# Weight groups multiplied by halves of the model's width over two PSUM banks, in a two-layer hybrid decoder step

## The chip, the cores and the metric

The kernel runs on one core of one Trainium2 chip. The metric is the device time of one execution in microseconds (us). TensorE (PE in the rows; its weight loads are PEld) multiplies into PSUM, VectorE (DVE), ScalarE (ACT) and GpSimd (POOL) do the elementwise work, and SyncE (SP) and ScalarE issue the DMAs.

## The reference

One inference step of a decoder with two layers. 2048 prompt tokens (one sequence) and 8 single sample tokens go through each layer with the same weights. Cut to what matters here:

```
hn   = rms_norm(x, norm_w)                     # (T, 1024)
proj = hn @ w_in                               # (T, 3336), split into 15 parts
       # r_q r_k r_v r_g | m_q m_k m_v m_o m_g m_i m_f | s_u s_g | a_q a_g   (256 wide; m_i, m_f 4 each)
ret  = head_norm(retention(rope(r_q), rope(r_k), r_v)) * silu(r_g)
ml   = head_norm(mlstm(m_q, m_k, m_v, m_i, m_f) * sigmoid(m_o)) * silu(m_g)
s5   = glu(gelu(s5_scan(s_u) + d * s_u)) * silu(s_g)
xa   = softmax(a_q @ mem_k.T / 8) @ mem_v * silu(a_g)
y    = x + concat(ret, ml, s5, xa) @ w_out     # (T, 1024)
# after the last layer: rms_norm(y, final_norm_w)
```

The outputs are y for prompt and sample tokens, the new recurrent states, and the memory keys and values. All is f32.

## The kernel before, in words

**Units and groups.** The prompt is cut into 4 units of 512 tokens, so there are 8 units in all (layer, unit). Each unit's normalised input stands transposed in SBUF as hT, the model's width on the partitions in 8 slices k of 128. The weights come in 140 groups of 256 columns (one, m_v, of 264), in an order written out by hand (ORDER and `wstream`): 4 groups for the memory, 13 projection groups for each unit, 4 groups of w_out (out0 to out3) for each unit, the last set of these by a function of its own (`out_last`).

**A group's weights.** `wload` brings a group as four quarters q0 to q3 of 256 rows (tiles wraw, four buffers, DMAs on SP's queue). `wsplit` makes of each quarter a rounded part whi on ScalarE and the rest wlo = wraw - whi, on VectorE for q0 and q2 and on GpSimd for q1 and q3. whi and wlo have WB = 6 buffers each: the four quarters of the current group and two of the next. `advance(i, 0)` loads group i+1 if that has not been done and splits its first half; `advance(i, 1)` splits its second half and loads group i+2.

**A group's matmuls.** A product takes three matmuls for each slice k: high with high, high with low, low with high. `tok_bank` puts tokens on the partitions (two token tiles of 128 in one PSUM bank; 256 columns each matmul, 96 matmuls for a group), `feat_bank` puts the group's columns on the partitions (512 tokens to a matmul, 48 for a group). In both, a bank takes all eight slices k, so q0 to q3 in turn, before the next bank m of the group begins. The banks pm come from a pool of four. After each bank its result is taken out of PSUM (`evac`, `evac_f`, or the add onto xr in `group_out`) and the function yields; then every open side chain makes one step (`step_sides`). Side chains (S5 scan, mLSTM, retention, attention, gates, norms) have four PSUM banks ps of their own and put their small matmuls and transposes between those of the groups.

**Unit b = 1 of each layer** carries the 8 sample tokens as well; there the feature groups run in two pieces of 260 columns. The last group of a unit is r_g; after each of its banks the next unit's input xt is transposed and split into hT (`hn_T`, two token tiles of 128 after each bank), and the next unit begins with m_v, whose banks take one token tile each.

**Who sets the order.** The program is written by the functions above, and a scheduler then places each engine's instructions in an order of its own; each engine runs its list strictly in that order. `group_out` before it starts makes side steps until all six parts of the unit's mix are there (mixd).

Of the kernel before, what the change touches and what calls it, by code (L numbers as in the profile page):

```python
# [7 lines left out]
F32 = mybir.dt.float32  # L8
# [4 lines left out]
OP = mybir.AluOpType  # L13
# [13 lines left out]
UT = 512  # L27
# [90 lines left out]
class Builder:  # L118
# [93 lines left out]
    def setup(self):  # L212
        nc, I, cp = self.nc, self.I, self.cp
        c = lambda n, s, dt=F32: cp.tile(s, dt, name=n, tag=n)
# [3 lines left out]
        self.mem_load()  # L218
        self.wload(0)
        self.hnl = self.hn_load(0, 0)  # L220
        next(self.hnl)
        self.wload(1)
        self.maskb = c("maskb", [128, 512], BF16)
# [84 lines left out]

    def wload(self, i):
        if i >= len(self.wseq) or i in self.wraw:  # L310
            return
        src, segs = self.wsegs(i)
        v = src.rearrange("(k p) c -> p k c", p=128)
        r = []
# [7 lines left out]
        self.wraw[i] = (r, o)  # L322

    def wsplit(self, i, half):
        if i >= len(self.wseq):
            return
        hi, lo, done = self.wspl.setdefault(i, ([], [], set()))
        if half in done:
            return
        done.add(half)  # L330
        r, n = self.wraw[i]
        for q in (2 * half, 2 * half + 1):
            hi.append(self.wp.tile([128, 2, 264], F32R, name=self.nm("whi"), tag="whi", bufs=WB))
            lo.append(self.wp.tile([128, 2, 264], F32R, name=self.nm("wlo"), tag="wlo", bufs=WB))
            h = hi[q][:, :, :n]
            self.act(h, r[q][:, :, :n])
            e = self.nc.gpsimd if q % 2 else self.nc.vector
            e.tensor_tensor(lo[q][:, :, :n], r[q][:, :, :n], h.bitcast(F32), OP.subtract)  # L338

# [48 lines left out]

    def tok_bank(self, tiles, n, hi, lo, aT, ps=None):

        ps = ps or self.mbank()
        for x, sl in enumerate(tiles):
            o = ps[:, x * n:(x + 1) * n]
            for k in range(8):
                a, c = aT(0, k, sl), aT(1, k, sl)
                h = hi[k // 2][:, k % 2, :n]
                self.mm(o, a, h, k == 0, False)
                self.mm(o, a, lo[k // 2][:, k % 2, :n], False, False)
                self.mm(o, c, h, False, k == 7)
        return ps  # L400

    def feat_bank(self, m, hi, lo, cols):

        ps = self.mbank()[:, :cols.stop - cols.start]
        for k in range(8):
            wh, wl = [x[k // 2][:, k % 2, m * 128:(m + 1) * 128] for x in (hi, lo)]
            self.mm(ps, wh, self.hT[0][:, k, cols], k == 0, False)
            self.mm(ps, wh, self.hT[1][:, k, cols], False, False)
            self.mm(ps, wl, self.hT[0][:, k, cols], False, k == 7)
        return ps  # L410
# [4 lines left out]
    def group(self, i):  # L415
        kind, l, b, g = self.wseq[i]
        if i == 0:
            self.wsplit(0, 0)
            self.wsplit(0, 1)
        hi, lo, _ = self.wspl[i]  # L420
        if kind == "mem":
# [10 lines left out]
        elif g in FEAT:  # L432
            if g == "r_q":
                for m in range(2):
                    self.u["rq", m] = self.g4([128, 2, UT], n="rqt")
                    self.dmaa(self.u["rq", m], self.I["c_rq"][b, m])
            smp = self.sample_in_unit(kind, l, b)
            pieces = [(0, 260), (260, 520)] if smp else [(0, UT)]
            for m in range(2):
                for c0, c1 in pieces:  # L440
                    ps = self.feat_bank(m, hi, lo, slice(c0, c1))
                    c2 = min(c1, UT)
                    self.evac_f(l, b, g, m, ps[:, :c2 - c0], slice(c0, c2))
# [6 lines left out]
                    if c1 >= UT and m == 1:  # L450
                        self.advance(i, 1)
                    yield
        else:
            if g == "m_v":
                jobs = [[t] for t in range(4)]
            else:
                jobs = [[0, 1], [2, 3]]
            n = 264 if g == "m_v" else 256
            for m, ts in enumerate(jobs):
                sls = [slice(t * 128, (t + 1) * 128) for t in ts]  # L460
                ps = self.tok_bank(sls, n, hi, lo, self.hslice)
                self.evac(l, b, g, m, ps)
                if m in (0, len(jobs) - 1):
                    self.advance(i, min(m, 1))
                if g == "r_g":
                    nxt = self.next_unit(l, b)
                    if nxt:
                        self.hn_T(2 * m)
                        self.hn_T(2 * m + 1)
# [4 lines left out]
    def advance(self, i, half):  # L474
        if half == 0:
            self.wload(i + 1)
            self.wsplit(i + 1, 0)
        else:
            self.wsplit(i + 1, 1)
            self.wload(i + 2)  # L480

# [236 lines left out]
    def gate_mix(self, u, l, b, src, g, br, gn, m):  # L718
# [6 lines left out]
        hi, lo = self.mix_tiles(u, br)  # L725
# [6 lines left out]
        for kk in range(2):  # L732
# [4 lines left out]
                                           h_.bitcast(F32), op0=OP.mult, op1=OP.subtract)  # L737
        u["mixd"] = u.get("mixd", 0) + 1

# [638 lines left out]
    def group_out(self, i, l, b, g, hi, lo):  # L1378
        v = self.nc.vector
        u = self.units[l, b]  # L1380
        while u.get("mixd", 0) < 6:
            n = u.get("mixd", 0)
            self.step_sides()
# [4 lines left out]

        if l == self.depth - 1 and b == self.NU - 1:
            yield from self.out_last(i, l, b, g, hi, lo, src, aT)  # L1390
            return
        for m in range(2):
            t0 = b * UT + m * 256
            xr = self.tb([128, 2, 256], "xr", bufs=2)
            rows = lambda a: a[t0:t0 + 256, g * 256:(g + 1) * 256].rearrange("(t p) c -> p t c", p=128)
            self.dma(xr, rows(src))
            ps = self.tok_bank([slice(t * 128, (t + 1) * 128) for t in (2 * m, 2 * m + 1)], 256, hi, lo, aT)
            v.tensor_tensor(xr, xr, ps.rearrange("p (t c) -> p t c", t=2), OP.add)  # L1398
            self.dma(rows(self.xd[l]), xr)
            self.advance(i, m)  # L1400
            yield
# [532 lines left out]
```

## Time and profile before

| what | value |
|---|---|
| median of 3 runs | 2450.93 us (2448.82 to 2454.46) |
| the profiled execution's own time | 2451.49 us |
| its span, first to last instruction | 2449.7 us |
| mean granted TensorE clock | 0.946 |
| busy: PE / PEld / DVE / ACT / POOL | 89% / 81% / 68% / 40% / 35% |
| mean DMA rate | 135 GB/s |

Busy PE counts the run-in and run-out of each pipelined matmul, so it stands above the time in which columns stream. The granted clock is 1.0 at 2.4 GHz and 0.5 at 1.2 GHz, and a mean of 0.946 mixes the two.

### The profile page before, as it was taken

The page shows a single profiled execution, that of the slowest core. Times are in us where ns is not written, and L with a number is a line of the kernel's source. Part 1 is how long each engine was busy: PE and PEld are TensorE (multiplying, and loading weights), DVE is VectorE, ACT ScalarE, POOL GpSimd, SP SyncE. Part 2 cuts the span into 40 slices and gives each one's busy share as a digit, 9 for nine tenths or more (in the row PEclk, how much of TensorE's full clock was granted, in tenths as well). Part 3 has the DMA queues.
Part 4 walks back from the last instruction along what each step waited for, and adds up shares of the span by engine and source line. Part 5 has one row for each costly group of instructions (what it writes and reads, how often), then busy time and mean ns, then how long its engine had stood idle before and what let it go on. Part 6 is the DMA issues. An engine that isn't in the chain of part 4 may idle for free.

```text
span 2449.7 us, 44181 instructions
## 1 busy us (share of the span) xinstructions
PE 2175.0 (89%) x16130; PEld 1989.2 (81%) x16130; DVE 1663.0 (68%) x4003; ACT 978.3 (40%) x2152; POOL 845.2 (35%) x755
## 2 busy tenths in 40 slices
PE   7899957897889989987889999878989899999898
PEld 6788856897788878875888889777989787888788
DVE  7987835646675789773874767347576678868474
ACT  4554423342433544243442454223443354433343
POOL 2443312232233435442322343213332244434243
PEclk9999988899999999998999999888999999999899
DMA  7525374447374435735435442784446643573522
GB/s 222 168 86 179 99 109 96 132 137 94 88 208 130 127 115 171 217 99 102 121 110 178 118 132 77 171 183 87 87 101 208 198 125 113 161 247 121 101 64 105
DMA packets 355529, 329.78 MB, mean 135 GB/s; under 512 B 109144, under 2 KB 310040, under 8 KB 355312
## 3 DMA queue, kind: packets, MB, share of 16 engines
q1 hardware_dynamic: 329472, 266.53, 43.2%
q10 hardware_dynamic: 25840, 60.43, 7.8%
q8 instruction: 127, 2.08, 0.4%
q14 instruction: 90, 0.74, 0.1%
HBM read 265.40 MB, written 45.73 MB: 127 GB/s over the span
## 4 chain that ended last, share of the span: by engine, by line
PE 34%; DVE 15%; DMA 14%; issue 3%; ACT 2%; SPq 2%; POOL 1%; ACTq 0%; DVEq 0%; POOLq 0%
PE pm L180 24%; PE ps L180 8%; DMA sv<-t 4%; DMA wraw<-w_in 3%; PE ps L184 2%; DVE wlo L338 2%; SPq L190 2%; DVE sm L207 1%; DVE t L1302 1%; DMA X<-ud 1%; DMA s5im_p<-xprev 1%; DVE sm L206 1%; DVE sm L208 1%; DMA ud<-U 1%; DVE sv L1297 1%
## 5 line engine op out<-in xcount | busy, mean ns | idle before, releaser
L338 POOL TENSOR_TENSOR wlo<-wraw,whi 128x512 fp32r<-128x512 f32 (+1 forms) x280 | 400.5, 1435 | 655.9 <-ACT whi L187 513.7
L180 PE MATMUL pm<-hT,whi 128*128 128x512 f32 (+1 forms) x2240 | 610.1, 361 | 5.3 <-ACT whi L187 5.3
L180 PE MATMUL pm<-whi,hT 128*128 128x256 f32 (+1 forms) x3072 | 593.4, 289 | 16.3 <-ACT whi L187 13.7
L180 PEld LDWEIGHTS pm<-whi,hT 128*128 128x128 f32 x3072 | 488.8, 193 | 23.1 <-ACT whi L187 14.3
L187 ACT ACTIVATE whi<-wraw 128x512 fp32r<-128x512 f32 (+1 forms) x560 | 342.2, 629 | 392.1 <-PE pm L180 250.2
L180 PE MATMUL pm<-wlo,hT 128*128 128x256 f32 (+1 forms) x1536 | 440.8, 288 | 28.3 <-DVE wlo L338 27.1
L180 PEld LDWEIGHTS pm<-hT,whi 128*128 128x128 f32 x2240 | 397.4, 194 | 64.5 <-ACT whi L187 5.7
L180 PE MATMUL pm<-hT,wlo 128*128 128x512 f32 (+1 forms) x1120 | 398.0, 359 | 25.7 <-DVE wlo L338 24.3
L180 PE MATMUL pm<-whi,mix 128*128 128x256 f32 x2048 | 382.1, 286 | 9.1 <-ACT whi L187 5.5
L338 DVE TENSOR_TENSOR wlo<-wraw,whi 128x512 fp32r<-128x512 f32 (+1 forms) x280 | 248.7, 891 | 153.2 <-ACT whi L187 130.7
L180 PEld LDWEIGHTS pm<-whi,mix 128*128 128x128 f32 x2048 | 324.3, 193 | 11.3 <-ACT whi L187 5.8
L180 PEld LDWEIGHTS pm<-wlo,hT 128*128 128x128 f32 x1536 | 295.7, 193 | 31.6 <-DVE wlo L338 28.9
L180 PE MATMUL pm<-wlo,mix 128*128 128x256 f32 x1024 | 292.7, 287 | 8.8 <-DVE wlo L338 8.8
L180 PEld LDWEIGHTS pm<-hT,wlo 128*128 128x128 f32 x1120 | 215.7, 193 | 59.4 <-DVE wlo L338 26.6
L180 PEld LDWEIGHTS pm<-wlo,mix 128*128 128x128 f32 x1024 | 197.5, 193 | 10.1 <-DVE wlo L338 9.8
L1310 POOL TENSOR_TENSOR t<-t,sCS 128x512 f32<-128x512 f32 x32 | 45.7, 1427 | 216.5 <-DVE t L1302 66.7
L187 ACT ACTIVATE Pt<-ps,sm 128x256 f32<-128x256 f32 x128 | 58.9, 472 | 129.6 <-DVE sm L951 123.4
L1297 DVE TENSOR_TENSOR sv<-sv,sCS 128x512 f32<-128x512 f32 x32 | 25.0, 782 | 99.6 <-DMA sv<-t 99.6
L959 POOL TENSOR_TENSOR Pt<-Pt,sm 128x512 f32<-128x512 f32 x32 | 46.3, 1448 | 56.3 <-DVE sm L957 40.7
L207 DVE SCALAR_TENSOR_TENSOR sm<-sm,sm 128x8 f32<-128x8 f32 (+4 forms) x210 | 60.5, 290 | 3.5
L1309 DVE TENSOR_TENSOR sv<-sv,sCS 128x512 f32<-128x512 f32 x32 | 26.8, 838 | 51.1 <-DMA sv<-t 51.0
L1398 DVE TENSOR_TENSOR xr<-xr,pm 128x512 f32<-128x512 f32 x56 | 37.9, 678 | 31.2 <-PE pm L180 23.1
(442 smaller groups left out, 3717.5 us busy)
## 6 DMA issues: line engine op xcount, KB each, us to landing
wraw<-w_in SPq DMA_DIRECT2D x416, 256.0 KB
wraw<-w_out SPq DMA_DIRECT2D x128, 256.0 KB
sCS<-CS SPq DMA_DIRECT2D x32, 512.0 KB
sv<-t SPq DMA_DIRECT2D x128, 128.0 KB
xd<-xr SPq DMA_DIRECT2D x56, 256.0 KB
xt<-x_prompt ACTq DMA_DIRECT2D x16, 512.0 KB
xr<-x_prompt SPq DMA_DIRECT2D x32, 256.0 KB
sWi<-Wi SPq DMA_DIRECT2D x32, 256.0 KB
```

The lines of the kernel that those rows point to most:

```text
L180: self.nc.tensor.matmul(out, lhsT, rhs, start=start, stop=stop, skip_group_check=skip)
L184: self.nc.tensor.transpose(out, in_, self.ident[:K, :K])
L187: self.nc.scalar.activation(out, in_, f, **kw)
L190: self.nc.sync.dma_start(out, in_)
L206: v.tensor_tensor(t, y, y, OP.mult)
L207: v.scalar_tensor_tensor(t, t, -0.5, b, op0=OP.mult, op1=OP.mult)
L338: e.tensor_tensor(lo[q][:, :, :n], r[q][:, :, :n], h.bitcast(F32), OP.subtract)
L959: e.tensor_tensor(Pt[:, 2 * x:2 * x + 2], Pt[:, 2 * x:2 * x + 2], sm_[:, 2 * x:2 * x + 2, None].to_broadcast([128, 2, MEM]), OP.mult)
L1297: v.tensor_tensor(Vs, Vs, Sn, OP.mult)
L1309: v.tensor_tensor(ys, ys, Sn, OP.mult)
L1310: gp.tensor_tensor(t1, y, Cs, OP.mult)
L1398: v.tensor_tensor(xr, xr, ps.rearrange("p (t c) -> p t c", t=2), OP.add)
```

## The change

110 of the 140 groups are multiplied in another order: both banks are taken at the group's start, both are filled with slices k = 0 to 3 (quarters q0 and q1), then both with k = 4 to 7 (q2 and q3). The results are taken out in the second half, each bank when it is complete. The other 30 keep whole banks: 4 for the memory, 8 m_v, the 14 feature groups of the sample units and the 4 of `out_last`. `advance(i, 0)` now stands at the group's start and splits the first half of group i+1 and loads the first half of i+2; `advance(i, 1)`, after the first half's matmuls, does the same with the second halves. `group_out` waits at its start for the retention and mLSTM parts of the mix alone (mixrm), and for the other two before its second half. Numbers of matmuls, splits, loads and side steps stay as they are.

```diff
-    def wload(self, i):
-        if i >= len(self.wseq) or i in self.wraw:
+    def wload(self, i, half):
+        if i >= len(self.wseq):
...
-        for q in range(4):
+        for q in (2 * half, 2 * half + 1):
             t = self.wp.tile([128, 2, 264], F32, name=self.nm("wraw"), tag="wraw", bufs=4)
...
+    def advance(self, i, half):
+        self.wsplit(i + 1, half)
+        self.wload(i + 2, half)
...
-            for k in range(8):
+            for k in ks:
                 a, c = aT(0, k, sl), aT(1, k, sl)
...
             smp = self.sample_in_unit(kind, l, b)
-            pieces = [(0, 260), (260, 520)] if smp else [(0, UT)]
+            if not smp:
+                ps = [self.mbank(), self.mbank()]
+                self.advance(i, 0)
+                for half in range(2):
+                    for m in range(2):
+                        self.feat_bank(m, hi, lo, slice(0, UT), ps[m], self.khalf(half))
+                        if half:
+                            self.evac_f(l, b, g, m, ps[m], slice(0, UT))
+                    if half == 0:
+                        self.advance(i, 1)
+                    yield
+                return
...
+            ps = [self.mbank(), self.mbank()]
+            self.advance(i, 0)
+            nxt = g == "r_g" and self.next_unit(l, b)
+            for half in range(2):
+                for m in range(2):
+                    self.tok_bank([slice(t * 128, (t + 1) * 128) for t in (2 * m, 2 * m + 1)], 256, hi, lo, self.hslice,
+                                  ps[m], self.khalf(half))
+                    if half:
+                        self.evac(l, b, g, m, ps[m])
+                        if nxt:
+                            self.hn_T(2 * m)
+                            self.hn_T(2 * m + 1)
+                if half == 0:
+                    self.advance(i, 1)
                 yield
...
-        if half == 0:
-            self.wload(i + 1)
-            self.wsplit(i + 1, 0)
-        else:
-            self.wsplit(i + 1, 1)
-            self.wload(i + 2)
...
-        while u.get("mixd", 0) < 6:
-            n = u.get("mixd", 0)
+        while u.get("mixrm", 0) < 4 or (last and u.get("mixd", 0) < 2):
             self.step_sides()
```

**Three places in the engines' lists.** The first is TensorE in group r_q of layer 0, unit 3. Before, pm_12929 and pm_13031 are the group's two banks, whi_12721 is q1, whi_12877 with wlo_12878 is q2, and whi_12717 is q0 (hT_149 and hT_150 are the high and low part of hT):

```order
L180 MATMUL pm_12929<-hT_149,whi_12721 128x512
L180 MATMUL pm_12929<-hT_150,whi_12721 128x512
L180 MATMUL pm_12929<-hT_149,wlo_12722 128x512
L180 MATMUL pm_12929<-hT_149,whi_12877 128x512
L180 MATMUL pm_12929<-hT_150,whi_12877 128x512
L180 MATMUL pm_13031<-hT_149,whi_12717 128x512
L180 MATMUL pm_12929<-hT_149,wlo_12878 128x512
```

Now the banks are pm_12929 and pm_12930, whi_12665 is q1 and whi_12661 is q0:

```order
L180 MATMUL pm_12929<-hT_149,whi_12665 128x512
L180 MATMUL pm_12929<-hT_150,whi_12665 128x512
L184 MATMUL ps_12893<-ident,cst_12894 64x128
L180 MATMUL pm_12929<-hT_149,wlo_12666 128x512
L180 MATMUL pm_12930<-hT_149,whi_12661 128x512
L180 MATMUL pm_12930<-hT_150,whi_12661 128x512
L180 MATMUL pm_12930<-hT_149,wlo_12662 128x512
```

Where the list went from q1 to q2 in one bank, it goes from q1 to q0 of the other bank, and q2 comes 12 matmuls later. In that second bank, ten matmuls on, the list has two transposes of Pt_12805 (attention weights).

The second place is VectorE at the same point of the program, around the MEMSET of xprev, the S5 state, which must wait until a DMA has read it out. Before:

```order
L705 TENSOR_TENSOR mh_11954<-mh_11954,sm_12772 128x512
L1231 TENSOR_TENSOR W_2294_12751<-W_2294_12751,w_2295_12752 128x320
L709 TENSOR_REDUCE sm_12778<-t_2298_12776 128x8
L1278 MEMSET xprev 128x16
L338 TENSOR_TENSOR wlo_12878<-wraw_12601,whi_12877 128x2x256
```

Now:

```order
L1294 MEMSET xprev 128x16
L208 SCALAR_TENSOR_TENSOR sm_12790<-sm_12791,sm_12790 128x8
L206 TENSOR_TENSOR sm_12791<-sm_12790 128x8
L207 SCALAR_TENSOR_TENSOR sm_12791<-sm_12791,sm_12788 128x8
L208 SCALAR_TENSOR_TENSOR sm_12790<-sm_12791,sm_12790 128x8
L973 RECIPROCAL sm_12807<-sm_12807 128x4
L975 TENSOR_TENSOR Pt_12805<-Pt_12805,sm_12807 128x512
L336 TENSOR_TENSOR wlo_12932<-wraw_12669,whi_12931 128x2x256
```

The split that stood right behind the MEMSET, of r_q's q2, now stands ahead of it, and the next one behind it, wlo_12932, is q0 of the following group; Pt_12805 is made behind the MEMSET.

The third place is TensorE at the end of layer 0, unit 2, where r_g ends and m_v of unit 3 begins (pm_10525 and pm_10408 are r_g's second banks before and now, pm_10624 is m_v's first bank, xt_10083 to xt_10089 are the four token tiles of the next input, xt_10097 to xt_10103 now). Before:

```order
L180 MATMUL pm_10418<-whi_10382,hT_150 128x256
L184 MATMUL ps_10478<-ident,xt_10083 128x128 x4
L184 MATMUL ps_10485<-ident,xt_10083 128x128 x4
L184 MATMUL ps_10492<-ident,xt_10085 128x128 x4
L180 MATMUL pm_10525<-whi_10378,hT_149 128x256
L180 MATMUL pm_10525<-wlo_10379,hT_149 128x256
```

Now:

```order
L180 MATMUL pm_10408<-wlo_10292,hT_149 128x256
L180 MATMUL pm_10408<-whi_10291,hT_150 128x256
L184 MATMUL ps_10492<-ident,mh_8616 128x128 x4
L184 MATMUL ps_10501<-ident,mh_8616 128x128 x4
L184 MATMUL ps_10537<-ident,xt_10097 128x128 x4
L184 MATMUL ps_10544<-ident,xt_10097 128x128 x4
L180 MATMUL pm_10624<-whi_10409,hT_149 128x264
L180 MATMUL pm_10624<-wlo_10410,hT_149 128x264
L184 MATMUL ps_10551<-ident,xt_10099 128x128 x4
L180 MATMUL pm_10624<-whi_10409,hT_150 128x264
```

Before, both transposes of the first token tile stood some 35 rows ahead of m_v; now they stand right at its start, and those of the second tile inside m_v's first bank. Of the seven boundaries between units four are changed in this way, before units 1 and 3 of either layer (in layer 1 the first tile keeps a lead of some 20 matmuls). Before unit 0 of layer 1 the transposes stood right at m_v's start already, and before unit 2 of either layer they stay ahead of it, by less than they did.

## Rows read from the trace of the kernel before

**Rows 1.** The page, busy time by engine; and the core's span and mean granted clock.

```profile
PE 2175.0 (89%) x16130; PEld 1989.2 (81%) x16130; DVE 1663.0 (68%) x4003; ACT 978.3 (40%) x2152; POOL 845.2 (35%) x755
core 0: 2449.7 us, clock 0.946
```

**Rows 2.** TensorE's waits in all: us in total, times, longest.

```profile
PE pm L180 <- DVE wlo L338: 60.5, 16, 18.0
PE pm L180 <- ACT whi L187: 26.2, 7, 11.1
PE ps L180 <- DVE xs L1311: 23.5, 4, 10.3
...
PE pm L180 <- POOL wlo L338: 4.4, 5, 1.8
```

**Rows 3.** Chain that ended last: start, us; one feature bank, one token bank.

```profile
1337.83 5.58 PE pm L180 x24
...
1352.46 5.66 PE pm L180 x48
```

**Rows 4.** The page's costliest groups: the three operations of a split.

```profile
L338 POOL TENSOR_TENSOR wlo<-wraw,whi 128x512 fp32r<-128x512 f32 (+1 forms) x280 | 400.5, 1435 | 655.9 <-ACT whi L187 513.7
...
L187 ACT ACTIVATE whi<-wraw 128x512 fp32r<-128x512 f32 (+1 forms) x560 | 342.2, 629 | 392.1 <-PE pm L180 250.2
...
L338 DVE TENSOR_TENSOR wlo<-wraw,whi 128x512 fp32r<-128x512 f32 (+1 forms) x280 | 248.7, 891 | 153.2 <-ACT whi L187 130.7
```

**Rows 5.** Timeline around 2217 to 2227 us, ScalarE, VectorE, TensorE.

```profile
2217.07 2.05 ACT L187 ACTIVATE whi<-wraw 128x512 fp32r<-128x512 f32 x3 [4.22 <-PE pm L180]
...
2225.85 0.68 DVE L338 TENSOR_TENSOR wlo<-wraw,whi 128x512 fp32r<-128x512 f32 x1
...
2226.59 0.51 PE L180 MATMUL pm<-hT,wlo 128*128 128x512 f32 x1 [3.95 <-DVE wlo L338]
```

**Rows 6.** Timeline: TensorE's three longest split waits, and what ended each.

```profile
591.38 1.06 ACT L187 ACTIVATE jk<-xt 128x1024 bf16<-128x1024 f32 x1 [10.07 <-DMA xt<-x_prompt]
...
596.21 0.79 PE L180 MATMUL pm<-whi,hT 128*128 128x256 f32 x2 [11.11 <-ACT whi L187]
...
620.22 0.17 DVE L1036 TENSOR_SCALAR sm<-sm 128x16 f32<-128x16 f32 x1 [9.27 <-DMA sm<-s_log_dt]
...
626.86 0.58 PE L180 MATMUL pm<-wlo,hT 128*128 128x256 f32 x1 [10.87 <-DVE wlo L338]
...
1129.20 0.69 DVE L338 TENSOR_TENSOR wlo<-wraw,whi 128x512 fp32r<-128x512 f32 x1 [21.48 <-DMA s5im_p<-xprev]
...
1129.95 0.79 PE L180 MATMUL pm<-hT,wlo 128*128 128x512 f32 x1 [18.04 <-DVE wlo L338]
```

**Rows 7.** Unit boundaries: length, busy PE, PEld, DVE, ACT, POOL, clock, DMA, GB/s.

```profile
900.00:930.00 30.00, 23.80 (x182) 22.77 (x183) 29.93 (x52) 12.63 (x24) 12.89 (x11) 0.94 0.32 89
1215.00:1245.00 30.00, 18.48 (x119) 16.78 (x119) 28.84 (x59) 15.41 (x32) 9.55 (x8) 0.77 0.18 55
1484.00:1506.00 22.00, 20.47 (x174) 20.10 (x173) 21.36 (x42) 10.88 (x23) 10.04 (x9) 1.00 0.28 74
...
2070.00:2100.00 30.00, 24.00 (x189) 23.62 (x190) 29.93 (x52) 13.65 (x26) 13.19 (x11) 0.94 0.33 89
```

**Rows 8.** TensorE's short split waits at boundaries: first and last of five.

```profile
PE pm L180 <- DVE wlo L338: 4.4, 1, 4.4
...
PE pm L180 <- DVE wlo L338: 4.2, 1, 4.2
```

**Rows 9.** TensorE's waits from 1215 to 1245 us.

```profile
PE ps L184 <- DVE xt L356: 4.5, 2, 3.2
PE ps L184 <- DVE hT L386: 3.8, 1, 3.8
```

**Rows 10.** Timeline: TensorE at the first matmul of the last w_out set.

```profile
2382.63 0.38 PE L180 MATMUL pm<-whi,mix 128*128 128x256 f32 x1 [2.70 <-ACT mix L187]
```

**Rows 11.** VectorE by line: the add that empties an output bank.

```profile
L1398 DVE TENSOR_TENSOR xr<-xr,pm 128x512 f32<-128x512 f32 x56 | 37.9, 678 | 31.2 <-PE pm L180 23.1 <-DMA xr<-x_prompt 3.8 <-DMA suT<-sproj 2.1
```

More of the change, by code (lines that the diff above doesn't have):

```diff
@@ L321, in wload @@
             r.append(t)
-        self.wraw[i] = (r, o)
     def wsplit(self, i, half):
@@ L326, in wsplit @@
             return
[L327 to L331, printed above, removed]
+        hi, lo = self.wspl.setdefault(i, ([], []))
+        n = sum(n for _, n in self.wsegs(i)[1])
         for q in (2 * half, 2 * half + 1):
@@ L449, in group @@
                         self.advance(i, 0)
-                    if c1 >= UT and m == 1:
+                    if c1 > UT and m == 1:
                         self.advance(i, 1)
                     yield
-        else:
-            if g == "m_v":
-                jobs = [[t] for t in range(4)]
-            else:
[L457 to L469, printed above, removed]
+        elif g == "m_v":
+            for m in range(4):
+                ps = self.tok_bank([slice(m * 128, (m + 1) * 128)], 264, hi, lo, self.hslice)
+                self.evac(l, b, g, m, ps)
+                if m in (0, 3):
+                    self.advance(i, m // 3)
+                yield
+        else:
+            ps = [self.mbank(), self.mbank()]
[12 more added lines that the diff above has]
+                    self.advance(i, 1)
                 yield
@@ L472, in group, with khalf @@
             self.sample_group(i, l, g, hi, lo, kind)
-    def advance(self, i, half):
-        if half == 0:
-            self.wload(i + 1)
-            self.wsplit(i + 1, 0)
-        else:
-            self.wsplit(i + 1, 1)
-            self.wload(i + 2)
+    def khalf(self, half):
+        return range(4 * half, 4 * half + 4)
     def next_unit(self, l, b):
@@ L737, in gate_mix @@
                                            h_.bitcast(F32), op0=OP.mult, op1=OP.subtract)
-        u["mixd"] = u.get("mixd", 0) + 1
+        u["mixrm"] = u.get("mixrm", 0) + 1
     def mk_T(self, u, m):
@@ L1380, in group_out @@
         u = self.units[l, b]
-        while u.get("mixd", 0) < 6:
-            n = u.get("mixd", 0)
+        last = l == self.depth - 1 and b == self.NU - 1
+        while u.get("mixrm", 0) < 4 or (last and u.get("mixd", 0) < 2):
             self.step_sides()
@@ L1387, in aT @@
             return u["mix", k // 2][w][:, k % 2, sl]
-        if l == self.depth - 1 and b == self.NU - 1:
+        if last:
             yield from self.out_last(i, l, b, g, hi, lo, src, aT)
             return
+        ps, xr = [self.mbank(), self.mbank()], []
+        rows = lambda a, m: a[b * UT + m * 256:b * UT + (m + 1) * 256, g * 256:(g + 1) * 256].rearrange("(t p) c -> p t c", p=128)
         for m in range(2):
[L1393 to L1400, printed above, removed]
+            xr.append(self.tb([128, 2, 256], "xr", bufs=2))
+            self.dma(xr[m], rows(src, m))
+        self.advance(i, 0)
+        for half in range(2):
+            while half and u.get("mixd", 0) < 2:
+                self.step_sides()
+            for m in range(2):
+                self.tok_bank([slice(t * 128, (t + 1) * 128) for t in (2 * m, 2 * m + 1)], 256, hi, lo, aT, ps[m],
+                              self.khalf(half))
+                if half:
+                    v.tensor_tensor(xr[m], xr[m], ps[m].rearrange("p (t c) -> p t c", t=2), OP.add)
+                    self.dma(rows(self.xd[l], m), xr[m])
+            if half == 0:
+                self.advance(i, 1)
             yield
```

38 lines of the change are left out of this document (21 added, 17 removed).

## The prediction

> **What bounds the kernel now.** I began with the page's busy times and the granted clock, then took TensorE's waits, the chain that ended last, and the timeline at the longest waits. TensorE is busy for 2175.0 of 2449.7 us [rows 1], so it stands idle for 274.7 us, and no other engine comes near its share; what can be gained lies in that idle time and in the clock. The reader is to see in [rows 2] that waits of the groups' matmuls for a split weight quarter (whi or wlo) come to 60.5 + 26.2 + 4.4 = 91.1 us in 28 waits, a third of the idle time; the side chains' waits make up most of the rest. A mean clock of 0.946 means that (1 - 0.946) x 2 = 10.8% of the span, 265 us, ran at 1.2 GHz.
>
> Why a split is late is seen from the pace. A feature bank takes 24 matmuls in 5.58 us and a token bank 48 in 5.66 us [rows 3], 0.2325 and 0.118 us each, so a group lasts about 11.2 us. With six buffers, q2 and q3 of the next group get the buffers that q0 and q1 of this one leave. Before, q0 is last read 18 matmuls before a group's end (4.2 us in a feature group's second bank, 2.1 us in a token group's last tile), and q2 of the next group is needed 12 matmuls into it (2.8 or 1.4 us). So between release and need lie 7.0 us or 3.5 us. A split takes 0.63 us on ScalarE and then 0.89 on VectorE or 1.44 on GpSimd [rows 4], 1.5 to 2.1 us, and whatever stands ahead of it in those engines' lists. [Rows 5] show an ordinary miss: ScalarE begins its splits at 2217.07, as soon as TensorE lets a buffer go, but VectorE comes to the wlo at 2225.85, and TensorE stands for 3.95 us.
>
> **The change part by part.** Number and length of the matmuls, splits and loads stay, so no busy time is removed: 0, hidden by nothing. What moves is the distance. In 110 groups q0 is last read 6 matmuls before the half, and q2 needed at the next one's half: 30 + 24 = 54 feature matmuls, 12.6 us, or 54 + 48 = 102 token matmuls, 12.0 us, so 5.6 or 8.5 us more.
>
> *Short split waits.* Without the three longest (18.0, 11.1 and 10.9, together 40.0 [rows 6]) 91.1 leaves 51.1 us in 25 waits, 2.0 us each on the mean. That is well below the distance added, so in halved groups they go as such. Two deductions: five of them, 14.2 us in all [rows 8], lie at unit boundaries where VectorE itself is busy for 29.93 of 30.00, 21.36 of 22.00 and 29.93 of 30.00 us [rows 7]; there it is the bound, and TensorE would only wait for it elsewhere. Of the other 36.9 us some lie in the memory and sample groups, which are not halved, and part comes back as waits of side chains, whose matmuls keep their places in TensorE's list, and whose DMAs take as long as before. Bounds: 0 and 36.9; I take three fifths, **-22**, since the 25 waits are scattered and the engines that were late were mostly busy, not blocked.
>
> *Long split waits.* Here an engine was held by a DMA [rows 6], and what matters is what TensorE meets next. At 1108 us VectorE waits 21.48 us for the DMA that reads xprev. The split behind that MEMSET moves ahead of it, but Pt_12805 is made behind it and is transposed 22 matmuls after r_q's start, so TensorE goes on for 1 to 3 us more and then waits as before: gain 2. At 591 us ScalarE waits for xt, with m_g's q2 in its list behind a sample group that isn't halved. TensorE then has 48 token matmuls before it needs q2 instead of 12, 36 x 0.118 = 4.2 us: gain 4. The next long wait, of r_g at 626.86, ends with VectorE's DMA for s_log_dt, whose landing doesn't move; it gives nothing more. Bounds 0 and 40; I take **-6**.
>
> *Clock.* If 28 of 275 us of idle time go, a tenth, and the 265 us at 1.2 GHz shrink likewise by 27, TensorE gains half of what it did in them, at most 13 us; part of those stretches was the wait itself. Bounds 0 and 13; **-5**.
>
> *Unit boundaries.* hn_T overwrites the hT slices that r_g's first bank reads. That bank used to be done at the group's half, and now at three quarters, 2.8 us later, so the next input's transposes crowd at m_v's start at four more boundaries. The boundary that already stands so is the one at 1215 us: TensorE is busy for 18.48 of 30 us at a clock of 0.77 [rows 7], and waits 4.5 and 3.8 us at these transposes [rows 9]. That one is also loaded with the new layer's constants, and at the others VectorE is the bound anyway. Bounds: 0, and 8.3 + 2 (its clock) at four, 41; I take 2 us at each, **+8**.
>
> *Tail.* The last r_g feeds the last w_out set at once: 2382.63 shows TensorE waiting 2.70 us for the mix [rows 10]. The first bank's gate starts a quarter of a group later, 11.3 / 4 = 2.8: **+3** (bounds 0 and 3).
>
> *Emptying banks.* Both results now fall in the last half of a group instead of one in each half. The add takes 0.68 us [rows 11] and the next group has two banks of its own, so it lies beside 11 us of matmuls: 0. If that cover were gone, it would cost one such operation for each of 110 groups, 75 us. The Trainium skill (Perfetto Trace Analysis, Optimizing Tensor Performance, Matmuls) says that independent groups of matmuls should go round the PSUM banks so that emptying one lies beside the next group's matmuls; this speaks against filling two side by side. By that rule as a cost of every group the sum would be 75 us worse; by the row and the four banks it is nothing.
>
> *Loads, the looser wait in group_out and the burst on SP's queue.* A quarter is now loaded about a group ahead of its split, as before, in two bursts instead of one; xr is still loaded a whole group after its previous store. 0, hidden by the 11.2 us between load and split; without that, a late load would show as ScalarE waiting for wraw.
>
> Sum: -22 - 6 - 5 + 8 + 3 = -22 us on the profiled execution's 2451.5, so 2429.5; that execution is 0.6 us above the median, which makes **2429 us**.
>
> **The rivals.**
> *All of it is kept.* The split waits go but for the boundaries, and the clock follows: -37 - 25 (the long ones, if other work fills them) - 13 + 3 = -72, 2379; with the boundaries' 14 us too, 2365. The case spans 2360 to 2409. For it: the waits are a third of TensorE's idle time. Against it: [rows 6], where a DMA sets the end.
> *No change.* TensorE comes early to side chains that end when they did: 3 us of the 22 are kept, and boundaries eat the rest; 2446 to 2456. For it: VectorE is full at the boundaries [rows 7], and side chains' waits outweigh the split waits.
> *Slower by the boundaries.* Each of the four changed ones costs as much as that at 1215 us, 10 us, and the two others 2: +44 + 3 against -33, 2465. It decides from (33 - 7) / 4 = 6.5 us a boundary on. For it: the order now there is that of the 1215 us boundary; against it: that one carries more on VectorE.
> *Banks are not emptied beside the matmuls:* +75 - 22, 2504. Against it: four banks.
>
> **How the numbers follow.** Forecast (2410 to 2444) 0.48, all kept 0.15, no change 0.14, slower by boundaries 0.19, banks 0.04. 0.2%, 5 us, is about what a measurement of this kernel can tell from no change. Faster is 0.48 + 0.15 = 0.63, same 0.14, slower 0.23. The range 2375 to 2467 leaves out under half of the case in which all is kept, and about half of the slower ones: 0.06 + 0.12. The forecast's own range is 2410 to 2444.
>
> **What would show it.** TensorE's waits for wlo from VectorE fall from 60.5 us to under 25, those for whi from 26.2 to about 10, of which m_g near 590 us is 7. Near 1108 us a wait of 15 us or more stands at ps<-ident,Pt in place of pm<-wlo. Waits at ps<-ident,xt and at m_v for hT rise by some 8 us over all boundaries; over 25 makes the slower rival right. The clock's mean rises to about 0.95. I am wrong if the split waits stay, if side chains' waits grow by as much as the splits' fall, or if adds and evacuations show TensorE waiting for a bank.

## The result, and the profile after

| | before | after |
|---|---|---|
| median | 2449.88 us (2440.67 to 2454.46, 4 runs) | 2474.16 us (2470.27 to 2481.01, 4 runs) |
| profiled execution, its own time | 2451.49 us | 2473.94 us |

The ratio is 1.0107, with a 95% interval from 1.007 to 1.0144: the change makes the kernel slower by about 1%, 45 us above the forecast and 7 us above the upper end of its range (2467).

The page of the changed kernel, busy time by engine, and the core's span with its mean granted clock, beside [rows 1]:

```profile
PE 2195.3 (89%) x16128; PEld 2012.6 (81%) x16130; DVE 1655.9 (67%) x4003; ACT 981.2 (40%) x2154; POOL 853.3 (35%) x755
core 0: 2472.2 us, clock 0.938
```

TensorE's idle time is 2472.2 - 2195.3 = 276.9 us, where it was 274.7. Its work is the same, but its busy time is 20.3 us longer, and the clock is lower: (1 - 0.938) x 2 x 2472.2 = 307 us at 1.2 GHz against 265, so TensorE, if it was busy through the 42 us more, lost half of them, 21 us. The whole difference of the spans, 22.5 us, is the 20.3 us and 2.2 us of idle time. This holds for these two executions alone: over all that are on record the mean clock of the kernel before is 0.945, in single ones 0.938 to 0.950, and that of the changed kernel 0.940 (0.938 to 0.942), so by the means the clock has a smaller share.

TensorE's waits in all (us in total, times, longest), beside [rows 2]:

```profile
PE ps L184 <- DVE Pt L975: 26.9, 8, 11.5
PE ps L184 <- DVE hT L388: 25.3, 6, 6.8
PE ps L180 <- DVE xs L1327: 21.1, 4, 10.1
PE ps L184 <- POOL mh L739: 20.9, 8, 8.6
PE ps L180 <- DVE E L877: 17.2, 8, 7.8
PE ps L180 <- POOL vw L880: 15.3, 4, 8.0
PE ps L180 <- DVE sm L840: 11.2, 5, 4.7
PE pm L180 <- ACT whi L187: 10.6, 6, 5.3
...
PE pm L180 <- DVE wlo L336: 5.6, 5, 2.0
...
PE pm L180 <- POOL wlo L336: 4.3, 3, 1.8
```

The three split rows fell from 91.1 to 20.5 us, as foreseen. In their place stand waits of matmuls into ps, the side chains' banks: Pt, mh, vw and hT had taken 1.9, 7.3, nothing and 8.9 us. From here on "split waits" are the sums of such pm rows for wlo and whi, and "side waits" the sums of the ps rows that VectorE, ScalarE or GpSimd ended: 136.4 us before, 216.8 now. So side waits grew by 80.4 us where split waits fell by 70.6, which is one of the signs that the prediction named for being wrong.

One of the new waits can be followed through three engines (timeline of the changed kernel near 1050 us, layer 0, unit 3; in brackets the idle time before and its releaser):

```profile
1045.31 9.55 SPq L190 DMA_DIRECT2D sv<-t  x3
...
1051.30 0.69 DVE L1313 TENSOR_TENSOR sv<-sv,sCS 128x512 f32<-128x512 f32 x1 [6.44 <-DMA sv<-t]
...
1052.76 1.61 DVE L1318 TENSOR_TENSOR_SCAN t<-ab,xprev,t 128x128 f32<-128x128 f32 x4
...
1054.50 2.17 POOL L1326 TENSOR_TENSOR t<-t,sCS 128x512 f32<-128x512 f32 x1 [10.34 <-DVE t L1318]
1056.64 1.90 POOL L1721 TENSOR_TENSOR sK<-sK,ssc 128x1024 f32<-128x1024 f32 x1
1058.49 1.26 POOL L336 TENSOR_TENSOR wlo<-wraw,whi 128x512 fp32r<-128x512 f32 x1
1059.71 1.48 POOL L1211 TENSOR_TENSOR cst<-js,sm 128x512 f32<-128x512 f32 x1
1061.16 0.62 POOL L880 TENSOR_TENSOR vw<-mv,RT 128x260 f32<-128x260 f32 x1
...
1061.83 0.70 PE L180 MATMUL ps<-vw,mkt 128*64 128x65 f32 x8 [7.97 <-POOL vw L880]
```

The reader is to see that vw, which TensorE wants for the mLSTM chain, stands in GpSimd's list behind t of another chain, the S5 scan, and that waits for a DMA by way of VectorE. With the loads alone in halves (below) vw stands behind the same t, but t waited 3.09 us there and not 10.34; vw was done 8 us before TensorE came to it, and the matmuls began without a wait:

```profile
1041.72 1.64 POOL L1337 TENSOR_TENSOR t<-t,sCS 128x512 f32<-128x512 f32 x1 [3.09 <-DVE t L1329]
...
1047.59 1.07 POOL L891 TENSOR_TENSOR vw<-mv,RT 128x260 f32<-128x260 f32 x1
...
1056.95 0.70 PE L181 MATMUL ps<-vw,mkt 128*64 128x65 f32 x8
```

At the boundary from unit 2 to 3 of layer 0, the waits of TensorE from 915 to 945 us, and the windows of that stretch and of the same boundary in layer 1 (columns as in [rows 7]):

```profile
PE ps L184 <- DVE hT L388: 6.8, 1, 6.8
PE ps L184 <- POOL mh L739: 6.4, 2, 5.9
915.00:945.00 30.00, 16.64 (x104) 15.35 (x104) 24.57 (x42) 9.48 (x18) 7.93 (x7) 0.72 0.15 44
...
2090.00:2120.00 30.00, 24.01 (x187) 23.23 (x186) 29.66 (x61) 13.80 (x28) 14.02 (x12) 0.94 0.29 80
```

### The profile page after: what moved, and what is told of

The parts are those of the page before. It is cut to its first block, busy times and chain, and to the rows that moved or that the text cites. A ratio compares the mean times of both kernels' runs of the same rounds, so it can differ in the third digit from the quotient of the medians.

```text
span 2472.2 us, 44160 instructions
## 1 busy us (share of the span) xinstructions
PE 2195.3 (89%) x16128; PEld 2012.6 (81%) x16130; DVE 1655.9 (67%) x4003; ACT 981.2 (40%) x2154; POOL 853.3 (35%) x755
## 4 chain that ended last, share of the span: by engine, by line
PE 44%; DVE 25%; DMA 17%; issue 5%; ACT 3%; SPq 3%; POOL 2%; ACTq 0%; another core or an unknown queue 0%; DVEq 0%; POOLq 0%
PE pm L180 32%; PE ps L180 10%; DMA sv<-t 7%; SPq L190 3%; PE ps L184 3%; DVE wlo L336 2%; DMA wraw<-w_in 2%; DVE t L1318 1%; DVE sm L208 1%; DVE sm L206 1%; DVE xt L358 1%; DVE sm L207 1%; DMA xd<-xr 1%; DMA sCS<-CS 1%; DVE aq L588 1%
## 5 line engine op out<-in xcount | busy, mean ns | idle before, releaser
L180 PE MATMUL pm<-whi,hT 128*128 128x256 f32 (+1 forms) x3072 | 603.9, 293 | 12.0 <-ACT whi L187 8.9
L187 ACT ACTIVATE whi<-wraw 128x512 fp32r<-128x512 f32 (+1 forms) x560 | 344.8, 631 | 473.8 <-PE pm L180 279.6
L180 PEld LDWEIGHTS pm<-whi,hT 128*128 128x128 f32 x3072 | 498.6, 196 | 19.0 <-ACT whi L187 9.9
L336 DVE TENSOR_TENSOR wlo<-wraw,whi 128x512 fp32r<-128x512 f32 (+1 forms) x280 | 232.2, 831 | 114.1 <-ACT whi L187 111.4
L180 PEld LDWEIGHTS pm<-wlo,hT 128*128 128x128 f32 x1536 | 301.2, 196 | 8.8 <-DVE wlo L336 5.0
L184 PE MATMUL ps<-ident,xt 128*128 128x128 f32 x256 | 41.2, 304 | 26.5 <-DVE hT L388 21.5
L208 DVE SCALAR_TENSOR_TENSOR sm<-sm,sm 128x8 f32<-128x8 f32 (+4 forms) x210 | 52.7, 252 | 17.9 <-DMA s5im_p<-xprev 13.9
```

The costliest lines, as they stand in the source:

```text
L180: self.nc.tensor.matmul(out, lhsT, rhs, start=start, stop=stop, skip_group_check=skip)
L184: self.nc.tensor.transpose(out, in_, self.ident[:K, :K])
L187: self.nc.scalar.activation(out, in_, f, **kw)
L208: v.scalar_tensor_tensor(y, t, 1.5, y, op0=OP.add, op1=OP.mult)
L336: e.tensor_tensor(lo[q][:, :, :n], r, h.bitcast(F32), OP.subtract)
```

## The experiments

All ratios are to the kernel before, run on the same chip; a per cent is 24.5 us. Three columns are from the profiled execution, in us.

| run | median us | ratio, 95% interval | split waits | side waits | idle |
|---|---|---|---|---|---|
| before | | 1 | 91.1 | 136.4 | 274.7 |
| after | 2474.16 | 1.0107 (1.007 to 1.0144) | 20.5 | 216.8 | 276.9 |
| e1 r_g by whole banks | 2471.56 | 1.0074 (1.0052 to 1.0096) | 34.6 | 212.8 | 284.7 |
| e2 loads alone | 2443.99 | 0.9958 (0.9937 to 0.9978) | 68.4 | 135.6 | 251.9 |
| e3 feature groups in halves | 2465.02 | 1.0053 (1.0036 to 1.0071) | 80.0 | 139.6 | 268.0 |
| e4 token and output groups | 2463.32 | 1.0037 (1.0015 to 1.0059) | 28.2 | 196.0 | 262.5 |
| e5 late emptying | 2483.75 | 1.0138 (1.0112 to 1.0165) | 53.9 | 180.6 | 281.6 |
| e6 steps at the quarters | 2476.75 | 1.0113 (1.0091 to 1.0134) | 30.4 | 190.2 | 283.6 |
| e7 loads, own xprev | 2439.32 | 0.9959 (0.9942 to 0.9977) | 77.0 | 134.9 | 259.5 |
| e8 after, own xprev | 2473.82 | 1.0101 (1.008 to 1.0123) | 18.8 | 220.7 | 278.2 |
| e9 steps amid the banks | 2480.78 | 1.0133 (1.0106 to 1.0159) | 58.4 | 148.7 | 275.5 |
| e10 later side work | 2465.33 | 1.007 (1.0048 to 1.0092) | 93.5 | 137.2 | 279.6 |
| e11 as e6, r_g whole | 2489.83 | 1.0166 (1.0142 to 1.019) | 36.6 | 194.5 | 288.7 |
| e12 output groups alone | 2452.91 | 1.0006 (0.9987 to 1.0024) | 59.8 | 163.5 | 268.2 |
| e13 15 buffers | 2452.39 | 1.0005 (0.9981 to 1.0029) | 68.7 | 137.4 | 264.3 |
| e14 15 buffers, WB 7 | 2454.4 | 0.9997 (0.9979 to 1.0015) | 38.7 | 167.2 | 269.3 |
| e15 15 and 9 buffers | 2456.75 | 1.0008 (0.9985 to 1.0031) | 57.5 | 147.1 | 262.0 |
| e16 15 and 9, WB 8 | 2453.8 | 1.0001 (0.998 to 1.0022) | 5.2 | 201.0 | 275.0 |
| e17 loads, short roots | 2401.03 | 0.9791 (0.9765 to 0.9816) | 58.3 | 132.5 | 230.1 |
| e18 after, short roots | 2432.2 | 0.9917 (0.9891 to 0.9942) | 18.8 | 193.0 | 250.3 |

**Where is the loss?** Theory A: the side chains set the pace, and split waits that go come back as side waits. Theory B: the boundaries lose it. The changed kernel with r_g bank by bank (e1), and with groups left out of the halves:

```diff
+        elif g not in HALVES:
...
+            for m in range(2):
+                ps = self.tok_bank([slice(t * 128, (t + 1) * 128) for t in (2 * m, 2 * m + 1)], 256, hi, lo, self.hslice)
+                self.evac(l, b, g, m, ps)
+                self.advance(i, m)
...
```

> The changed kernel (2474 us), with the last group of a unit, r_g, multiplied bank by bank again: its first bank ends at half of the group, and the transposes for the next unit start there. Theory A (side chains on VectorE, GpSimd and the transposes set the pace everywhere; the split waits that went came back as other waits, and the scattered waits cost clock): 2468 to 2478. Theory B (the loss sits at the seven unit boundaries, where the trace of the changed kernel falls about 15 us behind): 2455 to 2463, and the waits of TensorE on the transposes of xt and on hT at the boundaries go back to those of before.

> Loads and splits in halves as in the changed kernel, but every group multiplied bank by bank as before. Theories A and B both put the loss on the order of the multiplication: 2446 to 2456, as before, with split waits of about 80 to 90 us. A third theory, C, that the loads in halves themselves (the order of SyncE's queue) cost the time: 2465 to 2476.

> Only the feature groups (m_k, m_q, a_q, s_g, a_g, s_u, r_q) are multiplied in halves; token and output groups bank by bank. Theory A: about half of the split waits go and come back elsewhere, 2452 to 2464. Theory B: the boundaries are as before (r_g whole), so the gain of the split waits stays, 2430 to 2445.

> Only the token groups (m_o, r_k, r_v, m_g, r_g) and the output groups are multiplied in halves; feature groups bank by bank. Theory A: 2455 to 2468, the other part of the loss. Theory B: r_g is in halves, so the loss of the boundaries (15 us) stays and less is gained, 2462 to 2475.

Loads in halves alone don't lose, they gain 0.42% (C falls). Against that kernel, both kinds of groups lose when they are halved: feature groups 0.95%, token and output groups 0.79%, all 1.5%. In the kernels with halves the splits of the next group also stand half a group earlier in the program than with the loads alone (`advance(i, 0)` at its start); no run tried that by itself. Bringing r_g back gives 0.33%, some 8 us, with intervals that overlap: theory B explains about a fifth of it, and the median of e1 lies in the range of theory A. Nor did the waits at xt and hT go back to the 5.2 + 8.9 us of before, as theory B had them do; in e1 they are:

```profile
PE ps L185 <- DVE xt L359: 13.7, 5, 5.0
PE ps L185 <- DVE hT L389: 11.5, 8, 3.5
```

The feature groups lose without taking any split wait away (80.0 against 68.4 us), which neither theory had foreseen; their 2465.02 us lies just above both ranges.

> Loads in halves, and only the output groups multiplied in halves: their banks feed no side work but the store of the rows. Theory D: the split waits at the output groups go and nothing is late, 2434 to 2442. Theory A (what goes comes back on the side chains): 2442 to 2450. Theory E: no step is moved, 2436 to 2446.

e12's 2452.91 us is 0.48% above the loads alone, although these banks feed no side chain, and above what any of the theories allowed. Differences of this size can't be read, as the control e13 shows below.

**Is it the late emptying?** e5 keeps whole banks and holds back one matmul of the first bank, so that its emptying is late without halves. The side work that starts with that bank begins a step later with it, as it does in the changed kernel. e6 takes the changed kernel and moves the side steps:

```diff
 # e5
+                ms = self.keep(self.feat_bank, 0, hi, lo, slice(0, UT), ps[0])
+                self.issue(ms[:-1])
+                self.advance(i, 0)
+                yield
+                m1 = self.keep(self.feat_bank, 1, hi, lo, slice(0, UT), ps[1])
+                self.issue(m1[:12] + ms[-1:])
+                self.evac_f(l, b, g, 0, ps[0], slice(0, UT))
+                self.issue(m1[12:])
 # e6
                         self.feat_bank(m, hi, lo, slice(0, UT), ps[m], self.khalf(half))
                         if half:
                             self.evac_f(l, b, g, m, ps[m], slice(0, UT))
+                        if m == 0:
+                            yield
                     if half == 0:
                         self.advance(i, 1)
-                    yield
```

> Loads in halves and banks multiplied one after the other (the kernel of the run with loads alone, 2444 us), but in every feature and token group the last matmul of the first bank is kept back until half of the second, so that the first bank is emptied at three quarters of the group, as in the changed kernel; output groups as they were. Theory D (what costs the time is that the first bank is emptied a quarter of a group later, and just ahead of the second): 2458 to 2475. Theory A (the split waits that went came back elsewhere; when the banks are emptied does not matter): 2440 to 2450, since no split wait is taken away here.

> The changed kernel (2474 us) with the steps of the side work issued at one and at three quarters of each group and not at half and end, so that the first bank is emptied ahead of one step and the second ahead of the other, as before. Theory D: most of the loss comes back, 2440 to 2458. Theory A: 2468 to 2478.

e5 alone costs more than the whole change: 1.8% above the loads alone, 40 us by the medians, and more than the 2458 to 2475 us of theory D. But e6, which should have brought the loss back if it were the bunching at one step, brings nothing. So two more with whole banks: e9 yields amid each bank, and e10 empties the first bank in time but starts its side work a step later, with the second's:

```diff
 # e9
+                    self.feat_bank(m, hi, lo, slice(0, UT), ps, self.khalf(0))
+                    yield
+                    self.feat_bank(m, hi, lo, slice(0, UT), ps, self.khalf(1))
 # e10
-            self.sides.append(self.rk_T(u, m))
+            self.later(m, self.rk_T(u, m))      # m = 0: kept; m = 1: both are begun
```

> Loads in halves, banks multiplied one after the other and each emptied when it is done (the kernel of the run with loads alone, 2444 us), but the steps of the side work stand in the middle of each bank and not behind it. No bank is emptied later; only the place of the side steps is another, by a quarter of a group, as in the run with steps at the quarters (2477 us). Theory D (the late emptying costs): 2438 to 2450. Theory E (the side chains were laid out by hand for steps right behind each bank, and any other place of the steps costs about a per cent): 2465 to 2480.

> Loads in halves and banks emptied one after the other at half and end (2444 us), but the side work that begins with a group's first bank (the transposes of m_k and r_k, the gates of m_g and r_g) begins one step later, together with that of the second bank, as it does in the changed kernel. If this order of the side work is what the late emptying cost (theory F): 2462 to 2485. If it is the time at which the first bank's data is ready and its engines' queues are held (theory D): 2440 to 2452.

> Halves with the steps at the quarters (2477 us), and r_g bank by bank with its steps in the middle of its banks. Theory B (boundaries): 2455 to 2465, the waits on hT (23.6 us) back to about 10. Theory E: 2470 to 2480.

e9 loses 1.75% against the loads alone with no bank emptied late, just above what theory E allowed, and D is not needed for it; but there too the side work of a bank comes later in the program, by a quarter of a group. e10 loses 1.1%, within the range of F. Its side waits stay as they were (137.2 against 135.6 us), and the time stands in split waits (93.5 against 68.4): late side work can come back in either column. By theory B e11 should have come back to 2455 to 2465 with waits at hT of about 10 us; it is the slowest of all, with 25.3 us of them. e9 gives a reason why e6 did not help, that its place of the steps can be a loss by itself.

**Was there anything to gain?** The same split waits can be taken away with the groups' order as it was, by more buffers for whi and wlo; the memory comes from the side chains' pools, so each has a control that gives up as much:

```diff
-WB = 6
+WB = 8                                       # e14: 7
-        self.g4p = e(tc.tile_pool(name="g4p", bufs=16))
-        self.t2p = e(tc.tile_pool(name="t2p", bufs=11))
+        self.g4p = e(tc.tile_pool(name="g4p", bufs=15))
+        self.t2p = e(tc.tile_pool(name="t2p", bufs=9))     # e13, e14: 11
```

> Control for the next run: loads in halves alone (2444 us), with 15 buffers of 4 KB for the side work where there were 16. 2444 to 2460, by how often the side work needs the sixteenth; both theories alike.

> The control with 15 buffers, and 7 quarter buffers for split weights where there were 6: the third quarter of the next group is split without waiting for this group's last bank, no step of the side work moves, no bank is emptied later. Theory A (the side chains set the pace; split waits that go come back as other waits): within 6 us of the control, with split waits of some 20 to 35 us where the kernel with loads alone had 68 us. Theory G (the split waits bound, and the changed kernel lost only by its order): 25 to 45 us faster than the control.

> Control for the next run: loads in halves alone, with 15 buffers of 4 KB where there were 16 and 9 of 2 KB where there were 11. 2445 to 2480; both theories alike.

> The control with 15 and 9 buffers, and 8 quarter buffers for split weights: two whole groups, so that every split runs a whole group ahead. Theory A: within 8 us of the control, with split waits below 20 us. Theory G: 40 to 60 us faster than the control.

Theory G falls: e14 differs from its control by 2 us, e16 by -3 us, inside the intervals. (e14 kept 38.7 us of split waits, a little more than was expected.) TensorE's split waits in the control e15, and then all that is left of them in e16, with the two rows that grew most:

```profile
PE pm L181 <- DVE wlo L337: 37.1, 15, 11.8
...
PE pm L181 <- ACT whi L188: 14.9, 6, 9.0
...
PE pm L181 <- POOL wlo L337: 5.5, 6, 1.8
```

```profile
PE ps L185 <- POOL mh L750: 26.5, 4, 13.8
...
PE ps L181 <- POOL vw L891: 8.8, 3, 6.1
...
PE pm L181 <- ACT whi L188: 2.4, 2, 1.5
...
PE pm L181 <- POOL wlo L337: 2.0, 1, 2.0
...
PE pm L181 <- DVE wlo L337: 0.8, 1, 0.8
```

52.3 us of split waits went, 53.9 us of side waits came. The idle time of the profiled execution even rose, by 13.0 us, and its busy time fell by 14.9 (2195.5 to 2180.6) at the same clock of 0.941, so what is shown is that no time was gained, not where each microsecond went. One thing has to be taken back of what was expected: the program's order is the same in e14 and e13, but the scheduler placed some 1165 of TensorE's 13,029 rows elsewhere. e13 differs from e2 by one buffer and in the place of some 64 of those rows, and stands 0.47% higher; whether the buffer or the reshuffle does it is not told apart. Single effects below half a per cent (e1, e12, the gain of e2) are therefore not settled.

The longest wait of [rows 6] was tried by itself, with a tile xprev for each layer:

```diff
         if b == 0:
+            self.xprev = self.cp.tile([128, SG], F32, name=self.nm("xprev"), tag=f"xprev{l}", bufs=1)
             v.memset(self.xprev, 0.0)
```

> Loads in halves alone (2444 us) with an xprev of its own for each layer, so that VectorE's memset at the start of layer 1 waits for no DMA of the state (16.2 us in the trace with loads alone, behind which TensorE waited 13.4 us). If that wait sets the pace: 2430 to 2436. If the side chains catch up (theory A): 2440 to 2447.

> The changed kernel (2474 us) with an xprev of its own for each layer (VectorE waited 13.9 us there, TensorE 9.3 and 1.2 us behind it). If that wait sets the pace: 2462 to 2467. If the side chains catch up: 2470 to 2477.

VectorE's wait for that DMA (16.2 us with the loads alone, 13.9 us in the changed kernel) fell to nothing and to 0.5 us, and the ratios stay where they were, 0.9959 for 0.9958 and 1.0101 for 1.0107.

**Do the side chains set the pace?** VectorE's list alone is shortened:

```diff
-        for _ in range(3):
+        for _ in range(1):
             v.tensor_tensor(t, y, y, OP.mult)
```

> Loads in halves alone (2444 us), with one Newton step in each reciprocal square root where there were three: 420 of VectorE's 4003 instructions go (107 us of its busy time, by two thirds of the 160.9 us that those three lines take with loads alone), all of them in the norms of side chains, of rows and of the end; the result is a rougher root. No work of TensorE, no load and no split is touched. Theory A (the side chains set the pace): 2405 to 2430. If instead TensorE's own stream and its splits do: 2438 to 2446.

> The changed kernel (2474 us) with one Newton step where there were three (a rougher root), as in the run beside it. If the halves lose by making the side chains late (theories A and F): the loss against the run beside it shrinks from 30 us to 10 to 25, 2425 to 2450. If the halves cost TensorE something of its own: 30 us above the run beside it.

VectorE's list does set much of it: 43 us less than the loads alone (2401.03 against 2443.99), though no work of TensorE, no load and no split was touched, and by a little more than was expected. VectorE's splits stand in the same list and come earlier too (split waits 68.4 to 58.3 us, side waits 135.6 to 132.5), so the rows don't tell the chains from the splits; that removing split waits gave nothing (e14, e16) speaks for the chains. The page of e17:

```profile
PE 2169.6 (90%) x16130; PEld 1987.3 (83%) x16130; DVE 1596.6 (67%) x3583; ACT 979.2 (41%) x2152; POOL 852.6 (36%) x755
core 0: 2399.7 us, clock 0.956
```

Of the 43 us some 22 are idle time (251.9 to 230.1) and 21 busy time (2190.9 to 2169.6), with a higher clock (0.943 to 0.956). For e18 the expectation failed: it stands 31 us above e17, as the changed kernel stands 30 us above e2 (by the ratios 1.3% and 1.5%, which the intervals don't tell apart). That the halves' loss shrinks with VectorE's chains is not shown. Of the 31 us the idle time takes 20 (230.1 to 250.3) and busy time 11 at a lower clock (0.956 to 0.949), so it is waiting and clock, not more work of TensorE.

One row is largest with the halves and with the late first bank, and VectorE's shorter list leaves it as it was: the wait for vw, which GpSimd makes. It is 15.3 us in four waits in the changed kernel (above), two near 1060 and two near 2240 us, in the last unit of either layer. It stands at the same places in e5 and in e18:

```profile
PE ps L198 <- POOL vw L933: 15.9, 4, 6.4
```

```profile
PE ps L180 <- POOL vw L880: 15.7, 4, 8.1
```

e1 and e8 have it too (15.8 and 17.2 us). The kernel before, e2, e7, e9, e10, e13 and e15 have none of it, e12 and e17 0.2 and 1.2 us; the others, e14 and e16 with no late bank among them, have 5.3 to 8.8 us. So the changed kernel's loss may hang on GpSimd's list more than on VectorE's; no run shortened that list, and a row of waits alone is no cost, so this is not shown.

## Why the prediction was wrong

**Short split waits, -22, and long ones, -6.** The mechanism was right: wlo from VectorE fell to 5.6 us (under 25 was foreseen), whi to 10.6 (about 10). The step that failed is "I take three fifths": as far as the runs tell, nothing was kept. It rested on the waits being scattered and the late engines "mostly busy, not blocked", and took that for slack. It means the contrary: an engine that is late because it is busy is just as late for the next thing that TensorE wants from it. e16 shows it without the halves: 52 us of split waits gone, 54 us of side waits come, no time gained. Nor was the 18.0 us wait worth the 2 us. Near 1108 us TensorE now waits 9.3 + 1.2 us for Pt, where 15 or more was foreseen, and taking the cause away altogether changed nothing (e7, e8).

**Emptying banks, 0.** This step failed too, and by the experiments it is the one most likely to have made the kernel slower. What was priced was the add of 0.68 us and whether a bank is free; no wait of TensorE for a bank appears, so that much held. What hangs on the emptying was not priced: the side work that starts with the first bank's result, which comes a quarter of a group later and a step later in the program. Without halves, late emptying and the later step that goes with it cost 1.8% against the loads alone (e5) and the later step alone 1.1% (e10); the change costs 1.5%, 36 us, where the term was 0. That e9 loses as much with each bank emptied in time says that the place of the side work among the banks counts by itself. That these 36 us are the same loss is concluded from the three runs and not measured: e6, which should have given it back, did not, and the earlier place of the splits was not tried alone.

**Clock, -5.** The sign was wrong, since the idle time it was to follow did not shrink: 42 us more at 1.2 GHz in the profiled execution, up to 21 us lost.

**Unit boundaries, +8.** Of the right size, as far as can be told. TensorE's waits at xt and hT rose from 5.2 + 8.9 us (in the view of [rows 2]) to 2.9 + 25.3, by 14, and the groups' waits for hT from 0.2 to 2.2, below the 25 that would have made that rival right; r_g by whole banks gives back some 8 us, not settled, with those waits still at 13.7 + 11.5 us. The stretch from 915 to 945 us above (16.64 us busy, a clock of 0.72) is worse than that at 1215 us was in [rows 7], and with r_g by whole banks TensorE is busy there for 27.79 us at 0.89; the same boundary in layer 1 costs nothing, 24.01 us at 0.94 as before.

**Tail, +3.** The first matmul of the last w_out set waits for little now, but the transposes ahead of it wait for ro: 2.91 + 0.56 us where [rows 10] had 2.70, so +0.8.

```profile
2404.17 0.66 PE L184 MATMUL ps<-ident,ro 128*128 128x128 f32 x4 [2.91 <-POOL ro L739]
2405.39 0.39 PE L180 MATMUL pm<-whi,mix 128*128 128x256 f32 x1 [0.56 <-ACT mix L187]
```

**Loads, 0.** Earlier loads gained 0.42% (e2) and again 0.41% (e7), some 10 us; by the scatter that e13 shows this is at the edge of what can be told.

**The rivals.** "No change" had the right reason, that TensorE comes early to side chains that end when they did. "Slower by the boundaries" had the right sign for a reason that, by e1, is about a fifth of it. "Banks not emptied", where the rule of the Trainium skill was weighed (Perfetto Trace Analysis, Optimizing Tensor Performance, Matmuls), looked at the right operation: the rule asks that emptying lie beside other matmuls, and here it did, so no run shows its cost. The runs point to who waits for the emptied data instead.

**What stays open.** Moved side work and late banks cost 1.1 to 2.1% against the loads alone in six forms (after, e5, e6, e9, e10, e11), but which chain carries it is not shown. The wait for vw is largest where all the first banks but those of the output groups are late, but e9 and e10 lose without it, and shorter chains on VectorE did not clearly lessen the halves' loss. Since the scheduler rewrites the lists with each edit, a part of it may belong to the lists that it found, not to the edit.

The fastest kernel with the reference's whole work is the one with loads in halves alone (0.9958), with or without its own xprev.

## What to carry to other kernels

A row of waits names what ended last, not what bounds: before reordering work to remove a class of waits, remove it in a cheaper way, with buffers, and see whether anything is gained. Where side chains of other engines run between a main stream's banks, price a new order of the stream by who consumes each bank and at which step, not by the operation that empties it. If shortening the side chains' engine gives time and removing the stream's own waits gives none, the work lies in the chains.

## What the runs showed of the hardware that was not expected

The mean granted clock does not follow from the idle time: 274.7 us of it went with 0.946 and 276.9 with 0.938, and 262.0 and 275.0 us (e15, e16) went both with 0.941. The same program varies by itself: in some hundred executions of the kernel before the mean clock was 0.938 to 0.950, the time 2440 to 2469 us, the longer times at the lower clocks on the whole.

Of VectorE's time, taking out 420 small operations gave back 65.5 us (1662.1 to 1596.6) and not the 107 us that their share of the line sums promised. A line's mean mixes shapes, so the lines are shown by shape, with three steps and with one. The 128x8 operations that stayed took about what they had taken (234 to 240 ns, then 194 to 246); the 128x2 ones got longer (282 to 360 ns, then 362 to 582):

```profile
L207 DVE TENSOR_TENSOR sm<-sm 128x8 f32<-128x8 f32 x96 | 22.4, 234 | 2.5
...
L208 DVE SCALAR_TENSOR_TENSOR sm<-sm,sm 128x2 f32<-128x2 f32 x51 | 18.1, 360 | 0.5
```

```profile
L208 DVE SCALAR_TENSOR_TENSOR sm<-sm,sm 128x2 f32<-128x2 f32 x17 | 9.9, 582 | 0.1
...
L207 DVE TENSOR_TENSOR sm<-sm 128x8 f32<-128x8 f32 x32 | 7.9, 246 | 1.0
```

The three lines' sum fell by 97.5 us (160.9 to 63.4) where the engine's busy time fell by 65.5. By the records of both traces some 20 of the 32 us between were time in which these operations lay beside others on the engine, and some 12 us went to the other lines, whose time rose: a sum over lines is more than what their removal gives.
